# Nearest-neighbour upsampling by two: the first rows loaded in eight DMAs of 16 partitions

## The chip, the cores and the metric

The kernel runs on one core of a Trainium2 chip. The time is the device time in microseconds (us); three runs of the kernel before took 197.07, 197.08 and 197.4 us, so the median is 197.08. The engines that matter here are SP (SyncE), which only issues DMAs, VectorE (DVE), which copies inside SBUF, and the 16 DMA engines that move bytes between HBM and SBUF. POOL (GpSimd) takes part only in the barriers and in clearing the semaphores at the end.

## The reference

An input of 16 x 64 x 64 x 64 float32 is enlarged by two in both directions: every value appears four times in the output.

```python
batch, channels, h, w = (16, 64, 64, 64)
for i in range(new_h):
    for j in range(new_w):
        src_i = i // scale_factor
        src_j = j // scale_factor
        result[:, :, i, j] = x[:, :, src_i, src_j].copy()
```

The input has 16.78 MB, the output 67.11 MB. There is no arithmetic: bytes are read, repeated and written.

## The kernel before

All 16 x 64 x 64 = 65,536 image rows are spread over 128 partitions, R = 512 consecutive rows of 64 values (256 B) on each. One partition's part of the input is 128 KB in one piece of HBM, its part of the output 512 KB in one piece.

A single SBUF tile `mem` holds everything. Its back part, `xt`, is the whole input, 512 rows per partition (lines 143 and 144); its front part is free space, WF = 79 x 4 x 64 elements. The output is made in nine tiles of 62, 32, 48, 64, 50, 64, 64, 64 and 64 rows (`rows`, line 137). Tiles with an even number are written at the front of `mem`; tiles with an odd number are written so that they end exactly where their own input rows begin, over input that has been used up (line 162). So only two output tiles are alive at a time, and a copy into the third has to wait until the store of the first has landed.

Per tile, one DVE copy (line 170) writes each input value four times, with a broadcast over the two rows and the two columns, and one DMA from SP's queue (line 171) stores the tile; a tile of 62 rows is 7936 KB over 128 partitions. The first tile is copied in two halves of 31 rows.

The input comes in by the loop at lines 148 to 151, in three DMAs over all 128 partitions: rows 0 to 7 (HEAD = 8), rows 8 to 255, rows 256 to 511. Each piece is contiguous within a partition, so a load is one packet per partition. All loads and stores go out on SP's one queue, in the order in which SP issues them.

Two functions rewrite the finished program. `begin_before_barrier` takes the first EARLY DMAs of SP, which must wait for nothing, and puts them ahead of the barrier with which the engines start; before, EARLY = 3, which is all loads. `close_early` rearranges the end, so that the closing barrier and most of the semaphore clearing run while the last store is still under way, and SP's last instruction waits only for that store.

What orders the work is therefore: SP's program order for the DMAs, semaphores from loads to copies, from copies to stores, and from stores to the copies that use their place again. Semaphores of DMAs are used in turn, eight of them.

Of the kernel before, what the change touches and what calls it, by code (L numbers as in the profile page):

```python
# [1 line left out]

# [4 lines left out]

EARLY = 3  # L10


def begin_before_barrier(nc):

    blocks = nc.main_func.blocks
    main, body = blocks[0], blocks[1]
    sp = mybir.EngineType.SP
    loads = [i for i in body.instructions if i.engine == sp][:EARLY]  # L20
    for load in loads:
        assert isinstance(load, mybir.InstDMACopy), type(load)
        assert not (load.sync_info and load.sync_info.on_wait)
    names = [i.name for i in loads]
    body.instructions = [i for i in body.instructions if i.name not in names]
    kept = list(main.instructions)
    at = next(
        n
        for n, i in enumerate(kept)
        if i.engine == sp and isinstance(i, mybir.InstDrain)  # L30
    )
    kept[at:at] = loads
    main.instructions = kept


def close_early(nc):

    blocks = nc.main_func.blocks  # L40
    sp, pool = mybir.EngineType.SP, mybir.EngineType.Pool
    stores = [
        i
        for i in blocks[1].instructions
        if i.engine == sp and isinstance(i, mybir.InstDMACopy)
    ]
    last = stores[-1].sync_info.on_update[0].id

    end = list(blocks[-1].instructions)
    wait = end[0]  # L50
    assert wait.engine == sp and isinstance(wait, mybir.InstDrain)
    waits = list(wait.sync_info.on_wait)
    assert len({w.id for w in waits}) == len(waits) > 2
    assert all(w.wait_mode == "sem-ge-imm" for w in waits)

    mine = [i for i in end if i.engine == pool]
    kinds = [type(i).__name__ for i in mine]
    assert kinds == [
        "InstDrain",
        "InstEventSemaphore",  # L60
        "InstEventSemaphore",
        "InstDrain",
        "InstISA",
        "InstDrain",
        "InstEventSemaphore",
        "InstEventSemaphore",
    ], kinds
    d0, gather0, release0, d1, clear, d2, gather1, release1 = mine


    lo, hi = clear.ant_dict["range_first"], clear.ant_dict["range_last"]
    assert lo <= last <= hi and all(lo <= w.id <= hi for w in waits)
    clears = []
    for a, b in ((lo, last), (last + 1, hi + 1)):
        if a < b:
            clears.append(nc.gpsimd.sem_clear(range(a, b)).ins)

    landed = mybir.InstDrain(
        name=wait.name,
        engine=pool,  # L80
        debug=wait.debug,
        sync_info=mybir.SyncInfo(
            on_wait=[w for w in waits if w.id != last], on_update=[]
        ),
    )
    (w,) = [w for w in waits if w.id == last]
    final = mybir.InstEventSemaphore(
        name=clear.name,
        engine=sp,
        debug=wait.debug,  # L90
        sync_info=mybir.SyncInfo(
            on_wait=[w],
            on_update=[
                mybir.SyncUpdate(
                    sync_type=w.sync_type,
                    id=w.id,
                    ant_name=w.ant_name,
                    update_mode="sem-sub-imm",
                    update_value=w.wait_value,
                )  # L100
            ],
        ),
    )
    others = [i for i in end if i.engine != pool and i is not wait]
    blocks[-1].instructions = others + [
        d0, gather0, release0, gather1, release1, d1, landed, *clears, d2, final
    ]


@with_exitstack  # L110
def kernel(
    ctx: ExitStack,
    tc: tile.TileContext,
    x: bass.AP,
    scale_factor: int,
    out: bass.AP,
):
    nc = tc.nc
    nc.at_finalize(begin_before_barrier)
    nc.at_finalize(close_early)  # L120
    P = nc.NUM_PARTITIONS
    s = int(scale_factor)
    B, C, H, W = x.shape
    R = B * C * H // P
    fdt = x.dtype

    xp = x.rearrange("b c h w -> (b c h) w").rearrange("(p r) w -> p r w", p=P)
    op = out.rearrange("b c (h hd) w -> (b c h) (hd w)", hd=s).rearrange(  # L130
        "(p r) w -> p r w", p=P
    )

    rows = [62, 32, 48, 64, 50, 64, 64, 64, 64]
    GROW = s * s
    FREE = 79
    WF = FREE * GROW * W  # L140
    assert sum(rows) == R
    mem_pool = ctx.enter_context(tc.tile_pool(name="mem", bufs=1))
    mem = mem_pool.tile([P, WF + R * W], fdt, name="mem")
    xt = mem[:, WF:].rearrange("p (r w) -> p r w", r=R)

    HEAD = 8
    cuts = [0, HEAD, R // 2, R]
    for lo, hi in zip(cuts, cuts[1:]):  # L150
        nc.sync.dma_start(out=xt[:, lo:hi], in_=xp[:, lo:hi])  # L151

    def expanded(r0, r1):
        return (
            xt[:, r0:r1].unsqueeze(2).unsqueeze(4).to_broadcast([P, r1 - r0, s, W, s])
        )

    r0 = 0
    before = (0, 0)
    for n, k in enumerate(rows):  # L160
        size = k * GROW * W
        at = 0 if n % 2 == 0 else WF + r0 * W - size
        assert at >= before[1] or at + size <= before[0]
        before = (at, at + size)
        u = mem[:, at : at + size].rearrange(
            "p (k a w b) -> p k a w b", k=k, a=s, w=W
        )
        parts = [0, 31, k] if n == 0 else [0, k]
        for a, b in zip(parts, parts[1:]):
            nc.vector.tensor_copy(out=u[:, a:b], in_=expanded(r0 + a, r0 + b))  # L170
        nc.sync.dma_start(out=op[:, r0 : r0 + k, :], in_=u)
        r0 += k


# [1 line left out]
_INS = ['x', 'scale_factor']  # L176
_OUTS = [((16, 64, 128, 128), 'float32')]

_NUMBERS = {'scale_factor': 2}


# [26 lines left out]
```

## Time and profile before

| | |
|---|---|
| median of three runs | 197.08 us |
| span of the profiled execution | 195.8 us |
| DVE busy | 78.0 us, 10 copies |
| DMA queue busy | 99.2% of 16 engines' span |
| bytes moved | 83.89 MB, mean 428 GB/s |

The profiled execution's own time is known only as its span, from its first to its last instruction; the runs were timed apart from it, and 1.28 us lie between the span and their median.

How such a page is read: a view of 40 slices gives the busy share of each engine in tenths; the view of stretches gives, for a piece of the span, how long each engine was busy and what the DMA engines moved; the chain of waits follows the last instruction back to what released it; groups of instructions show the count, the mean duration of one, and what ended the idle time ahead of them. Times in the trace count from the start of the span. L170 is line 170 of the kernel. "SPq" is the queue of SP, which issues the DMAs. A DMA's time to landing runs from its issue to the arrival of its last byte.

### The profile page before, as it was taken

Reading aid. Unit: us, or ns where it says so; the run is one execution under the profiler, and the core shown is the slowest. Engines: PE = TensorE matmul, PEld = TensorE weight load, DVE = VectorE, ACT = ScalarE, POOL = GpSimd, SP = SyncE. Lnnn points to the kernel's source line nnn. Section 1 sums busy time; section 2 is a strip of 40 time slices with the busy share of each in tenths; the row PEclk is TensorE's granted clock in tenths of the full one; section 3 lists DMA queues with packets and bytes.
Section 4 is the critical chain, followed back from the end, with each engine's and each line's share of the span. In section 5 each row is a group of like instructions: output and inputs, shape, how many; then the busy total and the mean of one; then the engine's idle time right before and its main releaser. Section 6 shows DMA issues by size and latency. Waiting matters only on the chain.

```text
span 195.8 us, 76 instructions
## 1 busy us (share of the span) xinstructions
DVE 78.0 (40%) x10; POOL 0.2 (0%) x4
## 2 busy tenths in 40 slices
DVE  0000599980007579085008907900890088000000
POOL 0000000000000000000000000000000000000000
DMA  9999999999999999899987989999999999999994
GB/s 456 415 428 415 428 428 428 428 415 415 415 415 428 428 482 482 375 469 495 469 384 345 502 348 455 442 469 482 469 442 428 428 428 442 428 428 428 428 428 214
DMA packets 1728, 83.89 MB, mean 428 GB/s; under 512 B 192, under 2 KB 192, under 8 KB 320
## 3 DMA queue, kind: packets, MB, share of 16 engines
q1 hardware_dynamic: 1728, 83.89, 99.2%
HBM read 16.78 MB, written 67.11 MB: 428 GB/s over the span
## 4 chain that ended last, share of the span: by engine, by line
DMA 60%; DVE 24%; SPq 0%; issue 0%; DVEq 0%
DMA out_dram<-mem 49%; DVE mem L170 24%; DMA mem<-in_x_dram 11%; SPq L151 0%; DVEq L170 0%
## 5 line engine op out<-in xcount | busy, mean ns | idle before, releaser
L170 DVE COPY mem<-mem 128x16384 f32<-128x16384 f32 (+4 forms) x10 | 78.0, 7812 | 87.8 <-DMA out_dram<-mem 65.8
L189 POOL MEMSET const-uint8-127<- 128x1 uint8 x1 | 0.1, 102 | 0.0
L189 POOL MEMSET const-bfloat16-1.0<- 128x1 bf16 x1 | 0.1, 101 | 0.0
L189 POOL MEMSET const-float32-0.0<- 128x1 f32 x1 | 0.1, 98 | 0.2 <-issue 0.2
L189 POOL MEMSET const-float32-1.0<- 128x1 f32 x1 | 0.1, 98 | 0.0
## 6 DMA issues: line engine op xcount, KB each, us to landing
mem<-in_x_dram SPq DMA_DIRECT2D x1, 7936.0 KB, 21.5
out_dram<-mem SPq DMA_DIRECT2D x1, 7936.0 KB, 21.2
out_dram<-mem SPq DMA_DIRECT2D x1, 6400.0 KB, 27.6
out_dram<-mem SPq DMA_DIRECT2D x1, 6144.0 KB, 17.5
out_dram<-mem SPq DMA_DIRECT2D x1, 4096.0 KB, 26.4
mem<-in_x_dram SPq DMA_DIRECT2D x1, 256.0 KB, 2.7
out_dram<-mem SPq DMA_DIRECT2D x5, 29.8
mem<-in_x_dram SPq DMA_DIRECT2D x1, 40.4
```

The source lines that it names most:

```text
L170: nc.vector.tensor_copy(out=u[:, a:b], in_=expanded(r0 + a, r0 + b))
L189: nc = _bacc.Bacc("TRN2", target_bir_lowering=False, num_devices=1)
```

## The change

The load of the first rows is cut differently. The first 64 rows of each partition come in eight DMAs; the DMA with number q serves the 16 partitions q, q + 8, ..., q + 120, with 16 KB on each, 256 KB in all. Then rows 64 to 255 come in one DMA over 128 partitions, and rows 256 to 511 in another. EARLY rises from 3 to 8, so the eight small ones go ahead of the starting barrier and the two large ones come behind it.

```diff
-EARLY = 3
+EARLY = 8
...
-    HEAD = 8
-    cuts = [0, HEAD, R // 2, R]
-    for lo, hi in zip(cuts, cuts[1:]):
-        nc.sync.dma_start(out=xt[:, lo:hi], in_=xp[:, lo:hi])
+    HEAD = 64
+    for q in range(8):
+        group = slice(q, P, 8)
+        nc.sync.dma_start(out=xt[group, :HEAD], in_=xp[group, :HEAD])
+    nc.sync.dma_start(out=xt[:, HEAD : R // 2], in_=xp[:, HEAD : R // 2])
+    nc.sync.dma_start(out=xt[:, R // 2 :], in_=xp[:, R // 2 :])
```

Copies, stores and their places in SBUF are the same. With ten loads and eight semaphores for DMAs, the ninth and tenth load use the semaphores of the first and second again.

## The prediction

> **What bounds the kernel now.** I read the page's slices first, then its queue part, then the stretches of time, and only then the chain of waits.
>
> ```profile
> span 195.8 us, 76 instructions
> DVE 78.0 (40%) x10; POOL 0.2 (0%) x4
> DMA  9999999999999999899987989999999999999994
> q1 hardware_dynamic: 1728, 83.89, 99.2%
> HBM read 16.78 MB, written 67.11 MB: 428 GB/s over the span
> DMA packets 1728, 83.89 MB, mean 428 GB/s; under 512 B 192, under 2 KB 192, under 8 KB 320
> ```
>
> VectorE (DVE) works 40% of the span; the one DMA queue works 99.2% of it. The next rows are stretches of time (start and end, length, DVE and POOL busy, PE clock, DMA share, GB/s). A share above 1 only means that a packet counts where it starts.
>
> ```profile
> 0.00:1.00 1.00, 0.00 (x0) 0.20 (x4) 1.00 0.03 2
> 5.50:19.53 14.03, 0.00 (x0) 0.00 (x0) 1.00 1.00 434
> 22.20:36.68 14.48, 14.48 (x2) 0.00 (x0) 1.00 1.00 434
> 36.00:48.00 12.00, 7.17 (x2) 0.00 (x0) 1.00 1.00 431
> 129.00:153.15 24.15, 8.70 (x1) 0.00 (x0) 1.00 1.00 434
> 163.00:187.14 24.14, 2.88 (x1) 0.00 (x0) 1.00 1.00 434
> ```
>
> Loads (5.5 to 36.7 us) and stores (129 to 187 us) run at the same 434 GB/s, with and without a copy beside them. At that rate 83.89 MB take 83.89 / 0.434 = 193.3 us, so all that isn't streaming is 195.8 - 193.3 = 2.5 us. No change of order can gain more than that, and whatever slows a part of the stream adds to the end one for one.
>
> The chain of waits names copies too, but they don't set the end:
>
> ```profile
> 0.43 21.46 DMA mem<-in_x_dram
> 21.99 16.76 DVE mem L170 x2
> 38.77 21.19 DMA out_dram<-mem
> ```
>
> While the chain runs through the two copies, the row for 22.2 to 36.7 us shows the third load streaming at the full 434 GB/s. The span is counted as a queue of bytes.
>
> **The change part by part.** *The early copies.* Rows 0 to 63 of every partition are 128 x 64 x 256 B = 2.10 MB. They now arrive first, so the two 31-row copies no longer wait for rows 8 to 255.
>
> ```profile
> DVE mem L170 <- DMA out_dram<-mem: 65.8, 7, 16.8
> DVE mem L170 <- DMA mem<-in_x_dram: 22.0, 1, 22.0
> L170 DVE COPY mem<-mem 128x7936 f32<-128x7936 f32 x2 | 16.7, 8414 | 22.0 <-DMA mem<-in_x_dram 22.0
> ```
>
> 2.10 MB at 434 GB/s are 4.83 us. A start of 2.1 us (below) puts the first copy at about 6.9 us instead of 22.0 and the first store's issue at 6.9 + 16.8 = 23.7 us instead of 38.77. That store stands in one queue behind loads that stream until about 41 us either way. What it could fill is a hole between loads and stores. From 36 to 48 us the rate was 431: the lack is 12 x 3/434 = 0.08 us, so the gain lies between 0 and 0.1 us; I take 0. All later copies but the 32-row one wait for stores (65.8 us in 7 waits), and move with the queue. The 32-row copy needs rows 62 to 93 from the ninth load: 192 rows, 6.29 MB, 14.5 us, there at about 6.9 + 14.5 = 21.4 us, before DVE is free at 23.7. Were it late, its store is not wanted before the first store ends near 60 us: cost 0.
>
> *Issues on SP.* Three loads become ten; eight go out ahead of the barrier.
>
> ```profile
> 0.00 1.32 SPq L151 DMA_DIRECT2D mem<-in_x_dram  x3
> SPq L189 <- PEq L189: 0.2, 1, 0.2
> mem<-in_x_dram SPq DMA_DIRECT2D x1, 256.0 KB, 2.7
> mem<-in_x_dram SPq DMA_DIRECT2D x1, 7936.0 KB, 21.5
> mem<-in_x_dram SPq DMA_DIRECT2D x1, 40.4
> ```
>
> 1.32 us for three is 0.44 each, so eight take 3.5 us, and with a barrier of some 0.3 us (its wait was 0.2) the ninth is issued near 3.8 us. An issue of a smaller DMA was not seen; I bound it by 0 and by 0.44, and keep 0.44. In the first microsecond 0.03 of the DMA share is used, so bytes begin about 1.0 us after an issue: the ninth load is ready at 4.8 us. The eight early ones stream until 1.0 + 4.8 = 5.8 us or later. That is a cover of 1.0 us; without it each microsecond of delay on SP would cost one. In the compiled program the ninth load waits for the landing of the first early one, whose semaphore it uses again, and the tenth for the second. Those land at about 2.7 and 3.3 us, inside the issues; even at half the speed of streaming, about 3.3 and 4.5, the tenth isn't needed before the ninth's 14.5 us are through. Behind these waits on SP stand only stores due after 23 us. The other engines pass the barrier some 2.2 us later (five issues more before it), and DVE has nothing to do until 6.9. Cost 0.
>
> *Packets.* 1728 packets are 12 DMAs x 128 plus 192 under 512 B, that is 16 per DMA, one for each engine. With 19 DMAs that makes 7 more small ones per engine. If all 2.5 us outside the stream were the price of 12, seven would be 1.5 us; the stretch from 129 to 153 us crosses from one store to the next without falling below 434. Bounds 0 and 1.5; I take 0.
>
> *The seams between small DMAs.* The second load lands at 0.44 + 21.5 = 21.94 us, 19.24 after the first. Its 8.13 MB stream in 18.7, so 0.5 us were lost at the seam behind a small DMA. The third lands at 0.88 + 40.4 = 41.3, 19.3 later, with 8.39 MB in 19.3: nothing lost. Seven more seams cost 0 to 7 x 0.5 = 3.5 us. The first seam falls where the engines start up, so I take 0 for the middle and keep 3.5.
>
> *The shape of the early loads.* This is the term that decides. Every DMA of the trace touches all 128 partitions. Each early one touches 16, every eighth. If what holds 434 GB/s is the engines, all 16 still have a packet each and 2.10 MB cost 4.83 us as before. If it is the SBUF side, transfers that meet only every eighth partition may find only part of the ways in, and each sharing by two doubles the 4.83 us. The trace has the same 434 GB/s for loads, which read HBM, and for stores, which write it. So the limit lies in what both share, engines or the SBUF side, and not in HBM. Which of the two, no row tells. The bounds are +0 and, if every early DMA had to land before the next began, 8 x 2.7 - 4.83 = +16.8 us. That upper end is far: the second load came 19.24 us behind the first's landing, not 2.1 + 18.7 = 20.8. I take the smallest sharing, by two: +4.83 us. With the copies then starting at 11.8 us, the first store is issued at 28.5, still long before the loads end at 46.
>
> [...]
>
> *Sum.* Span 195.8 + 0 (copies) + 0 (issues) + 0 (packets) + 0 (seams) + 4.83 (shape) = 200.6 us. The median of the runs, 197.08, stands 1.28 above the profiled span; with the same distance: 201.9 us.
>
> **The rivals.** A is the forecast.
>
> B, nothing moves: the engines hold the rate, not SBUF. For it: 434 in every stretch, with one and the same packet order over 16 engines. The copies come early and the queue is just as long: 197.1 us, between 196.7 and 197.5. This is also the case in which the change does what it says and buys nothing.
>
> C, faster: the start shrinks. The first DMA lands at 2.7 us though its 0.26 MB stream in 0.6, so 2.1 us are start and landing. It hands each engine eight 2 KB packets (the 128 between "under 2 KB 192" and "under 8 KB 320"); now each engine gets one of 16 KB, and a DMA of 16 pieces may be ready sooner than one of 128. If half of the 2.1 us goes: 195.8 - 1.0 + 1.28 = 196.0 us. Against it: SP's issues took 0.33 to 0.43 us whatever they moved, and first bytes need their trip through HBM all the same. It decides if no sharing and no seam costs more than 0.6 us.
>
> ```profile
> L151 SPq DMA_DIRECT2D mem<-in_x_dram x3: 380/420/432, 0.0 to 0.9; - x3
> L171 SPq DMA_DIRECT2D out_dram<-mem x9: 332/332/348, 38.8 to 165.9; - x9
> ```
>
> D, the seams: no sharing, but each of seven new seams loses the 0.5 us of the first: 195.8 + 3.5 + 1.28 = 200.6 us. For it: the only seam behind a small DMA lost that. Against: the issues run 0.44 us apart and a packet train of 0.6, so work is always queued.
>
> **How the numbers follow.** A 0.53, D 0.14, B 0.18, C 0.15. A is ahead of B although the rows alone leave them even: the chance of a loss at the narrow shape takes in every degree of sharing, B only none. The predicted time is A's, 201.9; its own range is 200.6 (half of C's gain and a start partly hidden by the sharing) to 203.5 (A with half of the seams' 3.5). The range for eight in ten must reach down over B into C: 196.4 to 203.5. Left out are the best of C (0.07) and A with all seams or a sharing by more than two (0.1). About 0.2%, 0.4 us, is what a measurement of this kernel can tell from no change. Faster by more: C less its weak part, 0.15. Within: most of B, 0.17. Slower by more: A, D and the rest, 0.68.
>
> **What would show it.** Right: the first 10 to 12 us of the changed kernel run at about 217 GB/s instead of 434, the first copy starts near 12 us, the loads end near 46, and everything from the first store on is the old order shifted by 4 to 5 us. B: the first copy starts near 7 us, loads end at 41. C: bytes flow well before 1.0 us and the first store streams before 40. D: a copy start near 10 us with visible holes of half a microsecond between 16 KB packets, DMA share below 1. Wrong altogether would be a hole between the eighth and the ninth load (SP late), a DMA share under 0.9 after 12 us, or early loads served by fewer than 16 engines (fewer than 16 small packets per DMA).

## The result and the profile after

The changed kernel takes 202.02 us (201.92 to 202.15, 4 runs) against 197.1 for the kernel before: a ratio of 1.0244, with a 95% interval of 1.023 to 1.0259. It is slower by 4.9 us. Its profiled execution has a span of 200.6 us, 4.8 more than before.

The page of the changed kernel, the lines that answer to those of before:

```profile
span 200.6 us, 90 instructions
DVE 78.0 (39%) x10; POOL 0.2 (0%) x4
GB/s 183 216 372 431 470 418 418 418 431 494 506 405 327 451 418 470 470 366 431 457 523 379 480 337 581 418 418 418 418 418 418 418 418 418 418 457 470 536 418 209
DMA packets 1840, 83.89 MB, mean 418 GB/s; under 512 B 304, under 2 KB 304, under 8 KB 304
q1 hardware_dynamic: 1840, 83.89, 99.2%
```

The same bytes, the same 78.0 us of copies, and the DMA queue again 99.2% busy. Busy says nothing here of speed: the first two slices (5.0 us each) move 183 and 216 GB/s, and from the fourth on the kernel streams as before. The small packets are what the prediction counted, 19 x 16 = 304, beside 1536 large ones: 16 for each DMA, so by the prediction's reading (one for each engine) the narrow DMAs too run on all 16 engines. The DMA share of 1.01 in the first row below fits that. For the speed, the row of slices of the kernel before:

```profile
GB/s 456 415 428 415 428 428 428 428 415 415 415 415 428 428 482 482 375 469 495 469 384 345 502 348 455 442 469 482 469 442 428 428 428 442 428 428 428 428 428 214
```

Two stretches of the changed kernel (start and end, length, DVE and POOL busy, PE clock, DMA share, GB/s):

```profile
3.00:10.45 7.45, 0.00 (x0) 0.00 (x0) 1.00 1.01 211
133.80:157.95 24.15, 8.69 (x1) 0.00 (x0) 1.00 1.00 434
```

While the early loads run, the rate is 211 GB/s, less than half of 434; the stores of the later stretch have their old rate to the digit. The chain of waits and the timeline of the changed kernel (start, length, what) give the times at which things come:

```profile
4.41 7.90 DMA mem<-in_x_dram
12.43 16.76 DVE mem L172 x2
29.20 35.61 DMA out_dram<-mem
```

```profile
0.00 5.00 SPq L151 DMA_DIRECT2D mem<-in_x_dram  x8
5.65 0.35 SPq L152 DMA_DIRECT2D mem<-in_x_dram  x1
6.05 0.42 SPq L153 DMA_DIRECT2D mem<-in_x_dram  x1
```

The first copy starts at 12.43 us instead of 21.99, the first store is issued at 29.20 instead of 38.77, and none of it helps: that store lands at 64.81 us, where before it landed at 59.96. Every later step is the old one, 4.8 to 4.9 us late; the last copy, first before and then after:

```profile
157.19 8.69 DVE mem L170
```

```profile
161.96 8.69 DVE mem L172
```

### The profile page after: what moved, and what is told of

Read it like the earlier page. It is cut to its first block, busy times and chain, and to the rows that moved or that the text cites. A ratio compares the mean times of both kernels' runs of the same rounds, so it can differ in the third digit from the quotient of the medians.

```text
span 200.6 us, 90 instructions
## 1 busy us (share of the span) xinstructions
DVE 78.0 (39%) x10; POOL 0.2 (0%) x4
## 3 DMA queue, kind: packets, MB, share of 16 engines
q1 hardware_dynamic: 1840, 83.89, 99.2%
## 4 chain that ended last, share of the span: by engine, by line
DMA 59%; DVE 24%; SPq 2%; issue 0%; DVEq 0%
DMA out_dram<-mem 55%; DVE mem L172 24%; DMA mem<-in_x_dram 4%; SPq L151 2%; DVEq L172 0%
## 6 DMA issues: line engine op xcount, KB each, us to landing
mem<-in_x_dram SPq DMA_DIRECT2D x1, 6144.0 KB, 21.1
mem<-in_x_dram SPq DMA_DIRECT2D x1, 40.1
```

## The experiments

Three theories were put against each other. S: the narrow loads meet only part of the ways into SBUF, and engines that stand on one way share it. M: each small DMA costs a fixed time beside its bytes. H: HBM serves the address pattern of the narrow loads more slowly. Each diff is against the changed kernel unless the text says otherwise. EARLY, not shown, is set to the number of loads that wait for nothing: 3 with one early DMA, 4 with two, 8 with eight.

**The early rows in one DMA of 128 partitions.**

```diff
-    for q in range(8):
-        group = slice(q, P, 8)
-        nc.sync.dma_start(out=xt[group, :HEAD], in_=xp[group, :HEAD])
+    nc.sync.dma_start(out=xt[:, :HEAD], in_=xp[:, :HEAD])
```

> The early 64 rows in one DMA over all 128 partitions, all three loads ahead of the barrier. It keeps the early copies and takes the eight narrow DMAs away. Theory S (two DMA engines share one way into SBUF during the narrow loads): no sharing here, 197.1 us, between 196.8 and 197.4, and the first copy starts near 7 us. Theory M (each small DMA costs a fixed 0.6 us on top of its bytes, whatever its partitions): also 197.1. Theory H (HBM serves addresses 1 MB apart more slowly): also 197.1. If it stayed near 202, the early copies themselves would be the price (they would slow the loads), against all three.

Measured: 198.41 us, ratio 1.0058 (1.0045 to 1.0071). Most of the loss is gone, but the run is 1.2 us slower than before (its profiled span is 1.4 longer), which no theory said. The stretch of its early loads, and its DMAs (KB each, us from issue to landing):

```profile
2.70:6.35 3.65, 0.00 (x0) 0.00 (x0) 1.00 1.01 431
```

```profile
mem<-in_x_dram SPq DMA_DIRECT2D x1, 6144.0 KB, 21.4
mem<-in_x_dram SPq DMA_DIRECT2D x1, 2048.0 KB, 7.2
mem<-in_x_dram SPq DMA_DIRECT2D x1, 41.6
```

```profile
L150 SPq DMA_DIRECT2D mem<-in_x_dram x1: 424/424/424, 0.4 to 0.4; - x1
L151 SPq DMA_DIRECT2D mem<-in_x_dram x1: 432/432/432, 0.9 to 0.9; - x1
```

The early bytes come at 431 GB/s, so the 211 of the changed kernel belong to the narrow shape. The single packets that the traces keep say the same: one of 16 KB takes 0.61 us here at the median and 1.25 us in the changed kernel. The 1.2 us are lost later: the second load lands at 0.4 + 21.4 = 21.8 us, the third at 0.9 + 41.6 = 42.5, 20.7 us for 8.39 MB that stream in 19.3. The whole of it lies in the last 16 packets of 64 KB, which take 3.4 to 4.1 us each where the others take 2.42. In the changed kernel the ninth load lands at 5.65 + 21.1 = 26.75 and the tenth at 6.05 + 40.1 = 46.15, 19.4 us, nothing lost:

```profile
mem<-in_x_dram SPq DMA_DIRECT2D x1, 6144.0 KB, 21.1
mem<-in_x_dram SPq DMA_DIRECT2D x8, 256.0 KB, 5.8
mem<-in_x_dram SPq DMA_DIRECT2D x1, 40.1
```

**Two halves of 64 partitions.**

```diff
-    for q in range(8):
-        group = slice(q, P, 8)
+    for q in range(2):
+        group = slice(64 * q, 64 * q + 64)
         nc.sync.dma_start(out=xt[group, :HEAD], in_=xp[group, :HEAD])
```

> The early 64 rows in two DMAs, partitions 0 to 63 and 64 to 127, 1 MB each. [...] M: two small DMAs, 197.1 + 2 x 0.6 = 198.3 at most. [...]

Measured: 202.21 us, ratio 1.0248 (1.0233 to 1.0263), as slow as the changed kernel with two DMAs instead of eight. A stretch of its early loads:

```profile
3.30:10.80 7.50, 0.00 (x0) 0.00 (x0) 1.00 1.00 210
```

Again 210 GB/s, as on every eighth partition, and near half of 434: the sharing by two that S stands for fits here as well. M falls: two DMAs of 1 MB cost as much as eight small ones, 202.21 us where M has 198.3 at most. H, by which addresses 1 MB apart are the slow ones, misses too: the pieces of a half lie 128 KB apart in HBM.

**Sixteen neighbours.**

```diff
     for q in range(8):
-        group = slice(q, P, 8)
+        group = slice(16 * q, 16 * q + 16)
         nc.sync.dma_start(out=xt[group, :HEAD], in_=xp[group, :HEAD])
```

> Eight DMAs of 16 partitions as in the changed kernel, but 16 neighbouring ones each. [...] M: 202.0, as in the changed kernel. H: addresses 128 KB apart, if anything faster than the changed kernel, 197.1 to 202.

Measured: 208.74 us, ratio 1.0581 (1.0565 to 1.0598). The loss of 11.6 us is more than twice that of the changed kernel. It is against M, which has 202.0 for as many DMAs of the same size, and against H, which has at most 202. The stretch:

```profile
3.60:16.10 12.50, 0.00 (x0) 0.00 (x0) 1.00 1.01 126
```

126 GB/s is 126 / 434 = 0.29 of the full rate, less than the half that a sharing by two leaves. If engines share ways into SBUF, as S has it, more than two do so here; how many, the run doesn't show.

**A step of seven.**

```diff
-    for q in range(8):
-        group = slice(q, P, 8)
+    groups = [slice(q, q + 106, 7) for q in range(7)] + [slice(112, 128)]
+    for group in groups:
         nc.sync.dma_start(out=xt[group, :HEAD], in_=xp[group, :HEAD])
```

> Eight DMAs of 16 partitions, seven of them every seventh partition (from q = 0 to 6, partitions 0 to 111), the eighth partitions 112 to 127. [...] M: 202.0, as many DMAs of the same size. H: 896 KB apart instead of 1 MB: from 197.1 (if it is the power of two) to 202.

Measured: 202.24 us, ratio 1.0241 (1.0217 to 1.0264). The time is that of M, the trace is not:

```profile
2.24:8.05 5.81, 0.00 (x0) 0.00 (x0) 1.00 0.96 271
```

The seven DMAs with the step of seven move 271 GB/s, between the 211 of the step of eight and full speed (434). What they gain is lost again around the eighth DMA with its 16 neighbours: in the single packets of the trace, the last ones of 16 KB take up to 2.2 us, and the first wave of the large load behind them takes 2.3 to 4.5 us for packets of 48 KB that later take 1.82. By the time alone the run would speak for M, which the two halves rule out. For S the 271 says only that the step between the partitions counts; no run before had shown how much a step of seven shares.

**Source and destination crossed.** In one kernel each early DMA reads 16 neighbours' rows and writes every eighth partition, in the other the reverse; in both, rows 0 to 63 end in other partitions than they should.

```diff
     for q in range(8):
-        group = slice(q, P, 8)
-        nc.sync.dma_start(out=xt[group, :HEAD], in_=xp[group, :HEAD])
+        every, block = slice(q, P, 8), slice(16 * q, 16 * q + 16)
+        nc.sync.dma_start(out=xt[every, :HEAD], in_=xp[block, :HEAD])
...
+        nc.sync.dma_start(out=xt[block, :HEAD], in_=xp[every, :HEAD])
```

> As the changed kernel, but each early DMA reads 16 neighbouring partitions' rows from HBM (128 KB apart) and writes them to every eighth partition, so rows 0 to 63 of each partition hold other partitions' rows. S (sharing on the way into SBUF): only where the bytes go matters, so as in the changed kernel, 202.0 us. H (HBM serves some address patterns more slowly): the pattern is that of the run with 16 neighbours, so 208.7.

> The reverse: each early DMA reads every eighth partition's rows (1 MB apart) and writes 16 neighbouring partitions. S: as the run with 16 neighbours, 208.7 us, some 2.07 us for a packet of 16 KB. H: as the changed kernel, 202.0 us.

Measured: to every eighth partition 201.96 us, ratio 1.0239 (1.0204 to 1.0273); to a block 208.39 us, ratio 1.0555 (1.0519 to 1.0591). The stretch of the first, then of the second:

```profile
3.30:10.80 7.50, 0.00 (x0) 0.00 (x0) 1.00 1.00 210
```

```profile
3.55:16.00 12.45, 0.00 (x0) 0.00 (x0) 1.00 1.01 126
```

The rates go with the destination, whatever is read: 210 GB/s to every eighth partition, 126 to 16 neighbours. This settles it against H: the price is paid on the side of SBUF.

**Eight small DMAs of full width.**

```diff
-    for q in range(8):
-        group = slice(q, P, 8)
-        nc.sync.dma_start(out=xt[group, :HEAD], in_=xp[group, :HEAD])
+    for a in range(0, HEAD, 8):
+        nc.sync.dma_start(out=xt[:, a : a + 8], in_=xp[:, a : a + 8])
```

> Eight early DMAs of 256 KB ahead of the barrier as in the changed kernel, but each over all 128 partitions with 8 rows (packets of 2 KB). S: no narrow DMA, so full speed; at the start as the kernel before, 197.1, or as the run with one early DMA, 198.4, if what cost 1.3 us there (the last wave of load packets before the first store) comes back. M (a fixed cost for each small DMA, 0.5 to 0.6 us): 197.1 + 3.5 to 4.2 = 200.6 to 201.3.

Measured: 199.49 us, ratio 1.0125 (1.009 to 1.016), between S and M: +2.4 us.

```profile
2.50:6.90 4.40, 0.86 (x1) 0.00 (x0) 1.00 0.98 318
```

Its early loads, packets of 2 KB with seven more seams, move 318 GB/s: slower than one wide DMA (431), much faster than the narrow ones (211). 2.10 MB at 318 instead of 431 are 6.6 - 4.9 = 1.7 us, at most 0.25 for each seam, if all of it is the seams and none the small packets. Some of it is the packets: one of 2 KB takes 84 ns at the median, eight of them 0.67 us, where one of 16 KB took 0.61. The rest lies, as in the run with one early DMA, ahead of the first store; its two large loads:

```profile
mem<-in_x_dram SPq DMA_DIRECT2D x1, 6144.0 KB, 19.1
mem<-in_x_dram SPq DMA_DIRECT2D x1, 38.8
```

Issued at 4.1 and 4.5 us, they land at 23.2 and 43.3, 20.1 us apart instead of 19.3: 0.8 us lost.

**Twice the narrow rows.**

```diff
-    HEAD = 64
+    HEAD = 128
```

> The changed kernel with 128 instead of 64 rows in the eight narrow loads: 4.19 MB at the narrow speed, packets of 32 KB. S (a speed): the loss doubles, so 202.0 + 4.8 = 206.8 us, some 2.5 us for a packet. M (a fixed cost for each DMA): 202.0.

Measured: 207.61 us, ratio 1.0538 (1.0522 to 1.0553). The stretch of its early loads:

```profile
3.10:20.80 17.70, 0.00 (x0) 0.00 (x0) 1.00 1.00 207
```

The loss goes from 4.9 to 10.5 us: it grows with the bytes, a little more than double, so it is a speed and no price per DMA.

**The even and the odd partitions.**

```diff
-    for q in range(8):
-        group = slice(q, P, 8)
+    for q in range(2):
+        group = slice(q, P, 2)
         nc.sync.dma_start(out=xt[group, :HEAD], in_=xp[group, :HEAD])
```

> The early 64 rows in two DMAs of 64 partitions, the even ones and the odd ones. [...]

Measured: 198.77 us, ratio 1.0079 (1.0061 to 1.0097).

```profile
3.10:6.75 3.65, 0.00 (x0) 0.00 (x0) 1.00 1.01 431
```

The early loads are at full speed, with as many partitions and bytes per DMA as the two halves, which had 210. So it isn't the number of partitions: the two kernels differ only in which 64 partitions a DMA takes. Why the even and the odd ones keep the full rate, the run doesn't show. The time itself is 1.6 us above the kernel before: the late loss of the run with one early DMA is here again, with last load packets of 3.1 to 3.9 us.

**The late loss: when the first store is issued.** Two runs bear on the 1.2 us of the run with one early DMA. The first swaps its first two loads:

```diff
-    nc.sync.dma_start(out=xt[:, :HEAD], in_=xp[:, :HEAD])
     nc.sync.dma_start(out=xt[:, HEAD : R // 2], in_=xp[:, HEAD : R // 2])
+    nc.sync.dma_start(out=xt[:, :HEAD], in_=xp[:, :HEAD])
```

> The run with one early DMA of 64 rows took 198.4; its trace has 1.3 us lost in the last packets of the third load, which took 3.4 to 4.1 us instead of 2.42, with a store queued behind them since 24 us. Here the same three loads go out in another order: rows 64 to 255 first, then 0 to 63, then the rest, so the copies start near 22 us and the store is queued near 38.5, as in the kernel before. If the early store in the queue is what costs: 197.1. If the cut of the loads is what costs: 198.4.

Measured: 197.38 us, ratio 1.0008 (0.9994 to 1.0023): no difference from before, with the same three cuts. The second copies the first half tile twice:

```diff
+        if n == 0:
+            nc.vector.tensor_copy(out=u[:, :31], in_=expanded(0, 31))
         for a, b in zip(parts, parts[1:]):
```

> The run with one early DMA of 64 rows (198.4 us), with the first half of the first tile copied twice on DVE, so that the first store is issued 8.4 us later, near 32.4 instead of 24.0. If the time that a store stands behind the loads is what stretched their last packets: those packets are back at 2.42 us, 197.1. If it is that early loads and early copies come together at all: 198.4 still.

Measured: 198.37 us, ratio 1.0066 (1.0051 to 1.0081). Its third load still lands late:

```profile
mem<-in_x_dram SPq DMA_DIRECT2D x1, 41.5
```

Issued 0.9 us into the span, that is 42.4 us. So the loss comes with the first store queued at 24 or at 32 us and not at 38.7, just ahead of the last load's end; how long it waits in the queue doesn't matter between these. That a store behind the loads stretches their last packets is what fits, but it can't be the whole cause: the changed kernel has its store queued 17 us ahead of the loads' end and loses nothing there (its last load packets take 2.42 us). All four kernels with the loss have wide early loads, and none with narrow ones has it. This stays open.

**A narrow store.** The kernel before, with one store cut:

```diff
-        nc.sync.dma_start(out=op[:, r0 : r0 + k, :], in_=u)
+        if n == 1:
+            for q in range(8):
+                group = slice(q, P, 8)
+                nc.sync.dma_start(out=op[group, r0 : r0 + k, :], in_=u[group])
+        else:
+            nc.sync.dma_start(out=op[:, r0 : r0 + k, :], in_=u)
```

> The kernel before, but the store of the second tile (32 rows, 4.19 MB) is cut into eight DMAs of every eighth partition. If the sharing of theory S also holds for reads out of SBUF: 4.19 MB at half speed cost 9.7 us more, 206.8 us, and a packet of 32 KB takes some 2.5 us instead of 1.21. If only writes into SBUF share: 197.1 to 198.

Measured: 207.37 us, ratio 1.0523 (1.0506 to 1.0541).

```profile
60.60:77.10 16.50, 6.03 (x1) 0.00 (x0) 1.00 1.04 222
```

222 GB/s in the stretch of the narrow pieces, at a share of 1.04, and 2.5 us at the median for a packet of 32 KB instead of 1.21: reads out of SBUF by every eighth partition are slowed in the same way, and the 10.3 us are a little more than the 9.7 that doubling 4.19 MB gives.

## Why the prediction was right

**The bound.** A queue of bytes at 434 GB/s, in which a slow part adds to the end one for one. It held: the later stretch is at 434, and the whole difference lies in the first 13 us.

**The shape, +4.83 us.** This was the term that decided, and the choice between engines and SBUF side was not readable from the trace of before. The crossed runs show the SBUF side (210 or 126 GB/s, by the destination); the two runs with 64 partitions show that which partitions a DMA takes decides, at equal width (210 and 431 GB/s). HBM was ruled out too early in the prediction: loads and stores share HBM as well, so an equal 434 GB/s for both is no proof against it; the crossed runs are. The size was met within 3%: 211 GB/s against the 217 given. But the prediction took a sharing by two as the smallest step, not from a row: nothing in the trace of before shows a sharing, and as far as the rows of its trace go, that the size came out so near was luck. Nor does a halving hold for every narrow shape: 16 neighbours ran at 126 GB/s, the step of seven at 271. That engines share ways into SBUF remains a reading that fits; the runs show which partitions are slow, not the ways themselves.

**The copies, 0.** Right for this kernel, as the landing of the tenth load shows, but the bounds 0 to 0.1 us of gain were too narrow: with wide early loads the same early copies went with a loss of 1.2 us. An end below nothing was left out there.

**The issues on SP, 0.** Near the truth, by a working that was wrong. An issue with a step of eight takes longer than a wide one, not 0 to 0.44 us:

```profile
L151 SPq DMA_DIRECT2D mem<-in_x_dram x8: 571/589/589, 0.0 to 4.4; - x8
```

Eight took 5.0 us instead of 3.5, and the ninth load was issued at 5.65 instead of 3.8. The cover of 1.0 us would have been gone in rival B. It was the slow early loads themselves, the last of which lands at 4.41 + 7.90 = 12.31 us, that hid these issues. The first issue wasn't hidden: the first packet starts at 1.36 us instead of 1.00, and the first microsecond of the changed kernel moves nothing where the kernel before had begun.

```profile
0.00:1.00 1.00, 0.00 (x0) 0.20 (x4) 1.00 0.00 0
```

By the prediction's own rule such a delay adds to the end one for one. By this estimate some 0.4 of the 4.8 us are the later start and 4.4 the shape, and that the sum was met to 0.1 us is partly luck.

**The packets, 0,** and **the seams, 0 to 3.5.** The packet count came as predicted. Eight wide DMAs show at most 0.25 us for a seam, half of the 0.5 that rival D took; on the narrow loads none stands out beside the drop to 211 GB/s.

**The rivals.** B falls with 211 GB/s. C falls with the start: an issue of 0.58 us puts the first bytes later (1.36 us), not earlier. D falls with the two halves, which lose as much with two DMAs. Two of the prediction's figures don't follow from their working: C is given 0.15, and so is "C less its weak part"; and A with half of the seams' 3.5 us is 203.65, not 203.5.

## What to carry to other kernels

In a kernel that is bound by DMA, look at which partitions each DMA touches, not only at how many engines carry it: here 128 partitions or every second one ran at 431 to 434 GB/s, every eighth or one half at 210 to 211, 16 neighbours at 126, while the DMA share stayed near 1 in all. These are loads; the one narrow store tried, by every eighth partition, was slowed as much. So read GB/s by stretch beside the busy share. And an operation that starts ten microseconds earlier gains nothing where the queue behind it is already full: here the first copy started at 12.43 us instead of 21.99, and at 7.27 in the run with one early DMA, and neither kernel (202.02 and 198.41 us) ended before 197.1.

## What was not expected of the hardware

The time of a DMA's issue on SP isn't one size: 0.39 to 0.42 us for 16 neighbours in the runs that have only those, 0.55 to 0.59 for every eighth partition and for 64 partitions, whatever the source. The shape alone doesn't set it. In the run with the step of seven every early issue took 0.58 to 0.59 us, the eighth with its 16 neighbours too; and the large loads right behind the two halves took 0.59 and 0.74 us with all 128 partitions:

```profile
L151 SPq DMA_DIRECT2D mem<-in_x_dram x8: 578/589/589, 0.0 to 4.4; - x8
```

```profile
L152 SPq DMA_DIRECT2D mem<-in_x_dram x1: 585/585/585, 1.2 to 1.2; - x1
L153 SPq DMA_DIRECT2D mem<-in_x_dram x1: 739/739/739, 1.9 to 1.9; - x1
```

What sets it stays open. In the kernel with the narrow store most issues of the narrow pieces took about 1.35 us:

```profile
L174 SPq DMA_DIRECT2D out_dram<-mem x8: 492/1351/1363, 43.3 to 60.1; - x8
```

16 neighbours run at 126 / 210 = 0.6 of the speed of a half. A second sharing by two would have left 0.5; what sets the 0.6 no run shows. And the last load before the first store lost 0.8 to 1.4 us in some kernels with an early store and nothing in others, which no run here explains.
